# Decay products folded into q and k in place, in the scan of a three-branch decoder layer

## The chip, the cores and the metric

The kernel runs on one core of a Trainium2 chip, as one launch. The metric is the device time of that launch in microseconds (us). Three runs of the kernel before gave 2731.2, 2731.36 and 2727.7 us; the median is 2731.2 us. One more execution was recorded by the hardware profiler, and all rows of the trace come from it.

## The reference, cut to what matters

One layer over 2048 tokens (16 meta tokens stand ahead of them) with model width 1024. A normalised input goes through one wide projection, and three causal mixers run side by side on its parts: stick-breaking attention, a gated delta rule, and HGRN2, the third branch. Each has 4 heads of 128 dimensions; their outputs are gated, projected, mixed and added to the input. The change lies in the third branch, whose recurrence is, for one head and one chunk (`g_c` holds the running sum of the logarithms of the decays):

```python
o_inter = einsum('bhcd,bhde->bhce', q_c * exp(g_c), state)
dec = exp(where(causal, g_c[:, :, :, None, :] - g_c[:, :, None, :, :], -inf))
a = einsum('bhid,bhjd,bhijd->bhij', q_c, k_c, dec)
o = o_inter + einsum('bhij,bhje->bhie', a, v_c)
state = state * exp(g_end)[:, :, 0, :, None] + einsum('bhcd,bhce->bhde', k_c * exp(g_end - g_c), v_c)
```

The weight between token i and an earlier token j is thus a sum over 128 dimensions of q times k times the product of all decays between them, and each dimension has decays of its own.

## The kernel before, in words

The 2048 tokens are worked off in four stages of `TQ` = 512 (the loop over `j` at the end of the kernel). Dimensions lie on the 128 partitions and tokens along the free dimension, so a head's q is a tile of 128 x 528 (16 columns for the meta tokens of the first stage). The projections are made in three fp32r passes per product (`mm3`, lines 176 to 178): high part times high part and the two cross terms. They are by far the most of the work on TensorE.

Within a stage, two streams of work are traced one into the other by `weave`. One is the dense stream (`dense_work`): projections, gates and output products. The other is a scan: `sb_scan` (attention), `gdn_scan`, and `hg_scan` for the third branch, called twice per stage, for heads 0 and 1 and for heads 2 and 3. Here these are called the first and the second scan of a stage; there are eight in all. A scan yields an estimate of its own time (5.0 for each level of `hg_scan`), and `weave` traces dense work for a proportional time before it goes on with the scan. The program is traced under a context that orders the instructions of every engine along a simulated timeline; the order is fixed before the run, and each engine works through its own queue in that order. `issue_after` ties a block of instructions behind a given one on its engine.

`hg_scan` makes the 128 x 128 weight matrices by doubling. At level `s` = 1, 2, 4, ..., 64 the tokens are seen in pairs of neighbouring blocks of `s` tokens, a left one (k) and a right one (q). The weights between them need k times the decays from its token to the end of the left block, and q times the decays from the start of the right block to its token. For these:

- `pf` holds for every token the product of decays from the start of its block to itself, and `sf` the product from the token after it to the end of its block. Both are doubled in place after each level (line 1216 for `pf`, line 1215 for `sf`; at level 1 `sf` is made by GpSimd, lines 1212 and 1213).
- At each level a fresh tile `kql` from the pool "S" (21 buffers) takes right halves q times `pf` (line 1143) and left halves k times `sf` (line 1147; at level 1 a copy of k by GpSimd, line 1145).
- The level's products, 16 matmuls per head of 32 x 32 (levels 1 to 32) or 4 of 64 x 64, go into one bank `z` (line 1152), head 1 ahead of head 0. Level 1 has 16 more per head, k times q, for the diagonal.
- VectorE takes the wanted entries out of `z` by a mask (line 1200), and ScalarE copies them into `AT` (lines 1187, 1194 and 1207).

After the last level, q times `pf` (line 1223) and k times `sf` (line 1225) are made for whole chunks of 128, the latter is transposed on TensorE and copied by ScalarE (line 1227), and four steps per head run the recurrence between the chunks: lines 1236 to 1239 on TensorE, the update of the state on line 1241, the copy of the output on line 1242. The output goes on as `ob` to the product of the third branch.

Of the kernel before, what the change touches and what calls it, by code (L numbers as in the profile page):

```python
# [11 lines left out]
ALU = mybir.AluOpType  # L12
# [3 lines left out]
P = 128  # L16
# [3 lines left out]
META = 16  # L20
# [19 lines left out]
def kernel(  # L40
# [21 lines left out]
    nc = tc.nc  # L62
# [13 lines left out]
    def nm(s):  # L76
        uid[0] += 1
        return f"{s}_{uid[0]}"
# [5 lines left out]
    def slot(tag, shape=(P, WQ), dt=F32, bufs=None):  # L84
        return pool.tile(list(shape), dt, tag=tag, name=nm(tag), bufs=bufs or BUFS[tag])
# [18 lines left out]
    def p_z():  # L104
        return ps_z.tile([P, 512], F32, tag="z", name=nm("z"))

    def p_tr():
        return ps_z.tile([P, 512], F32, tag="z", name=nm("tr"))
# [20 lines left out]
    def rsqrt(v, rows, cols):  # L129

        y = slot("nr", (P, 24), F32, 4)
        u = slot("nu", (P, 24), F32, 4)
        nc.gpsimd.tensor_scalar(u[:rows, :cols], v, EPS, None, ALU.add)  # L133
        nc.gpsimd.tensor_tensor(y[:rows, :cols], u[:rows, :cols], mhalf[:rows, :cols], ALU.pow)
        return y
# [242 lines left out]
    def to_tokens(src, pt):  # L378

        for n in range(NT):  # L380
            nc.tensor.transpose(pt[:, n * P : (n + 1) * P], src[:, META + n * P : META + (n + 1) * P], ident)  # L381
        return pt
# [744 lines left out]
    def hg_scan(j, hs, st):  # L1127

        pf, kk, qq, vt, gate = zip(*(st.pop(h) for h in hs))
        two = range(2)  # L1130
        sf = [slot("S") for _ in two]
        s = 1
        lv = 0
        while s < P:
            def v4(t):
                r_ = t[:, META:].rearrange("p (b two s) -> p b two s", two=2, s=s)
                return r_[:, :, 0], r_[:, :, 1]

            nb = TQ // (2 * s)
            kql = [slot("S") for _ in two]  # L1140
            for i in two:
                kl_, kr_ = v4(kql[i])
                nc.vector.tensor_mul(kr_, v4(qq[i])[1], v4(pf[i])[1])
                if s == 1:
                    nc.gpsimd.tensor_copy(kl_, v4(kk[i])[0])
                else:
                    nc.vector.tensor_mul(kl_, v4(kk[i])[0], v4(sf[i])[0])
            z = p_z()
            last = None

            def mm(dst, lh, rh):
                return nc.tensor.matmul(dst, lh, rh, start=True, stop=True).ins  # L1152


            for i in (1, 0):
                with ExitStack() as es:
                    if last is not None:
                        es.enter_context(tc.issue_after(last))
                    if s == 64:

                        for n in range(NT):
                            c, o = META + n * P, 64 * (n % 2)
                            m = 2 * i + n // 2
                            last = mm(
                                z[o : o + 64, m * 64 : m * 64 + 64], kql[i][:, c : c + 64], kql[i][:, c + 64 : c + P]
                            )
                    elif s == 32:
                        for n in range(NT):
                            for b in (0, 64):
                                c, o = META + n * P + b, b + 32 * (n % 2)  # L1170
                                m = 2 * i + n // 2
                                last = mm(
                                    z[o : o + 32, m * 32 : m * 32 + 32], kql[i][:, c : c + 32],
                                    kql[i][:, c + 32 : c + 64],
                                )
                    else:

                        pairs = [(kql[i], kql[i])] + ([(kk[i], qq[i])] if s == 1 else [])
                        for q, (lh, rh) in enumerate(pairs):
                            for n in range(NT):  # L1180
                                for b in range(0, P, 32):
                                    c = META + n * P + b
                                    m = 2 * NT * q + NT * i + n
                                    last = mm(z[b : b + 32, m * 32 : m * 32 + 32], lh[:, c : c + 32], rh[:, c : c + 32])
            if s == 64:
                for g in two:
                    nc.scalar.copy(
                        AT[:64, :, g::2, 64:],
                        z[64 * g : 64 * g + 64, :256].rearrange("p (i n c) -> p i n c", i=2, n=2),
                    )  # L1190
            elif s == 32:
                for b in (0, 64):
                    for g in two:
                        nc.scalar.copy(
                            AT[b : b + 32, :, g::2, b + 32 : b + 64],
                            z[b + 32 * g : b + 32 * g + 32, :P].rearrange("p (i n c) -> p i n c", i=2, n=2),
                        )
            else:
                for q in range(2 if s == 1 else 1):
                    nc.vector.copy_predicated(  # L1200
                        AD, lvl[:, lv + 5 * q : lv + 5 * q + 1].broadcast_to([P, 2 * NT, 32]),
                        z[:, 256 * q : 256 * q + 256].rearrange("p (m c) -> p m c", c=32),
                    )
                if s == 16:
                    for b in range(4):
                        sl = slice(32 * b, 32 * b + 32)
                        nc.scalar.copy(AT[sl, :, :, sl], AD[sl].rearrange("p (i n) c -> p i n c", i=2))
            for i in two:
                pl_, pr_ = v4(pf[i])
                fl_, fr_ = v4(sf[i])  # L1210
                if s == 1:
                    nc.gpsimd.tensor_copy(fl_, pr_)
                    nc.gpsimd.memset(fr_, 1.0)
                else:
                    nc.vector.tensor_mul(fl_, fl_, pr_[:, :, s - 1 : s].broadcast_to([P, nb, s]))
                nc.vector.tensor_mul(pr_, pr_, pl_[:, :, s - 1 : s].broadcast_to([P, nb, s]))
            s *= 2
            lv += 1
            yield 5.0
        qe, ke, ket, os_ = [], [], [], []  # L1220
        for i in two:
            qe.append(slot("S"))
            nc.vector.tensor_mul(qe[i][:, META:], qq[i][:, META:], pf[i][:, META:])
            ke.append(slot("S"))
            nc.vector.tensor_mul(ke[i][:, META:], kk[i][:, META:], sf[i][:, META:])
            ket.append(slot("S", (P, NT, P)))
            nc.scalar.copy(ket[i].rearrange("p a b -> p (a b)"), to_tokens(ke[i], p_tr()))
            os_.append(slot("S"))
        ssq = slot("ssq", (P, 2 * NT), F32, 3)
        yield 4.0  # L1230
        for n in range(NT):
            cs = slice(META + n * P, META + (n + 1) * P)
            for i, h in enumerate(hs):
                p1 = p_tr()
                dst = p1[:, :P]
                nc.tensor.matmul(dst, qe[i][:, cs], Sh[h], start=True, stop=False)
                nc.tensor.matmul(dst, AT[:, i, n], vt[i][:, n], start=False, stop=True)  # L1237
                pS = p1[:, P : 2 * P]
                nc.tensor.matmul(pS, ket[i][:, n], vt[i][:, n], start=True, stop=True)
                e = META + (n + 1) * P - 1  # L1240
                nc.vector.scalar_tensor_tensor(Sh[h], Sh[h], pf[i][:, e : e + 1], pS, ALU.mult, ALU.add)
                nc.vector.tensor_copy(os_[i][:, cs], dst)
                junk = slot("junk", (P, P), F32, 2)
                m = NT * i + n
                nc.scalar.activation(
                    junk, os_[i][:, cs], AF.Square, scale=HD ** -0.5, accum_out=ssq[:, m : m + 1]
                )
                yield 1.5
        r = rsqrt(ssq, P, 2 * NT)
        yield 16.0  # L1250
        res = []
        for i in two:
            for n in range(NT):
                cs = slice(META + n * P, META + (n + 1) * P)
                m = NT * i + n
                nc.vector.tensor_scalar(os_[i][:, cs], os_[i][:, cs], r[:, m : m + 1], None, ALU.mult)
            res.append(put_ob(to_tokens(os_[i], p_tr()), gate[i]))
        return res
# [176 lines left out]
    with tc.issue_after(marks["act"]), tc.issue_after(marks["dve"]), tc.issue_after(marks["pool"]):  # L1435
# [47 lines left out]
        Sh = [const.tile([P, HD], F32, name=f"Sh{h}") for h in range(H)]  # L1483
# [123 lines left out]
```

## Time and profile before

| | |
|---|---|
| Profiled execution, device time | 2731.59 us |
| its span, first to last instruction | 2729.8 us |
| Median of three runs | 2731.2 us |
| TensorE matmul (PE) busy | 2693.7 us, 99% of the span |
| TensorE weight load (PEld) busy | 2245.8 us, 82% |
| VectorE (DVE) busy | 1433.1 us, 52% |
| ScalarE (ACT) busy | 960.2 us, 35% |
| GpSimd (POOL) busy | 718.8 us, 26% |
| Granted TensorE clock, mean | 0.998 |

Busy time is the time in which an engine has at least one instruction under way, so two that overlap count once; the mean of a group of instructions is that of their own durations. A row of a group ends with the idle time of its engine just ahead of it and with what ended that idle time. In rows that are ordered by time, the first number is the start and the second the length, both in us, and a number in square brackets is the idle time ahead.

### The profile page before, as it was taken

To read this page: it belongs to the slowest core of one execution; us is meant where nothing else is said; L and a number is where in the kernel's file an instruction comes from. 1 tells how busy PE (TensorE), PEld (TensorE's weight loads), DVE (VectorE), ACT (ScalarE), POOL (GpSimd) and SP (SyncE) were. 2 spreads that over 40 slices of the span, in tenths; PEclk is the share of its full clock that TensorE was granted. 3 is DMA by queue.
4 is the path that set the end of the run, shared out by engine and by line. 5 is a ranking of instruction groups with operands and counts; after the bars stand their busy time and mean duration, and the time that the engine had idled before them with its cause. 6 is when DMAs were issued, how large, how long until landed. Compare 5 with 4: busy or idle time off the path is not lost.

```text
span 2729.8 us, 46703 instructions
## 1 busy us (share of the span) xinstructions
PE 2693.7 (99%) x17984; PEld 2245.8 (82%) x17984; DVE 1433.1 (52%) x2878; ACT 960.2 (35%) x2207; POOL 718.8 (26%) x990
## 2 busy tenths in 40 slices
PE   7999999999999999999999999999999999999999
PEld 7998788888888888888888888888888887787887
DVE  5466647745357634443255765553325568556422
ACT  5564343343346212212144641321214456313120
POOL 4555213333133401112122332111212233302111
PEclk9999999999999999999999999999999999999999
DMA  7677756679654654557755456355764454554556
GB/s 261 221 235 251 250 184 221 231 268 319 197 180 146 206 176 130 157 160 242 230 188 171 156 171 203 107 156 155 253 217 142 163 169 142 161 161 121 162 162 212
DMA packets 201986, 521.08 MB, mean 191 GB/s; under 512 B 42976, under 2 KB 47008, under 8 KB 201764
## 3 DMA queue, kind: packets, MB, share of 16 engines
q1 hardware_dynamic: 201476, 518.03, 59.1%
q8 instruction: 142, 2.33, 0.3%
q14 instruction: 80, 0.66, 0.1%
q10 hardware_dynamic: 288, 0.07, 0.0%
HBM read 397.57 MB, written 120.44 MB: 190 GB/s over the span
## 4 chain that ended last, share of the span: by engine, by line
PE 93%; DVE 4%; DMA 1%; ACT 1%; issue 1%; POOL 0%; SPq 0%; DVEq 0%; POOLq 0%; ACTq 0%
PE acc L176 20%; PE acc L177 20%; PE acc L178 20%; PE av L176 5%; PE av L177 5%; PE av L178 5%; PE tr L559 2%; PE t L381 2%; PE z L1152 1%; PE z L176 1%; PE z L177 1%; PE z L178 1%; PE tr L381 1%; PE z L856 1%; PE tr L1237 1%
## 5 line engine op out<-in xcount | busy, mean ns | idle before, releaser
L176 PE MATMUL acc<-xh,w 128*128 128x512 f32 (+2 forms) x2096 | 796.8, 380 | 5.6 <-DVE y L1285 1.7
L177 PE MATMUL acc<-xl,w 128*128 128x512 f32 (+2 forms) x2096 | 790.7, 377 | 0.3 <-DVE xl L261 0.3
L178 PE MATMUL acc<-xh,w 128*128 128x512 f32 (+2 forms) x2096 | 787.1, 376 | 0.5 <-DVE w L127 0.5
L176 PEld LDWEIGHTS acc<-xh,w 128*128 128x128 f32 x2096 | 396.6, 189 | 75.2 <-DVE y L1285 2.1
L178 PEld LDWEIGHTS acc<-xh,w 128*128 128x128 f32 x2096 | 396.6, 189 | 66.8 <-DVE w L127 0.7
L177 PEld LDWEIGHTS acc<-xl,w 128*128 128x128 f32 x2096 | 396.4, 189 | 65.0 <-DVE xl L261 1.1
L531 DVE TENSOR_TENSOR_SCAN S<-S,zero 128x128 f32<-128x128 f32 (+4 forms) x216 | 199.1, 924 | 115.3 <-ACT S L525 105.1
L127 POOL TENSOR_TENSOR w<-wraw,w 128x512 fp32r<-128x512 f32 x106 | 147.0, 1390 | 236.2 <-ACT w L156 227.7
L537 POOL TENSOR_TENSOR S<-S,S 128x256 f32<-128x256 f32 (+2 forms) x108 | 96.5, 893 | 366.6 <-DVE S L531 196.6
L176 PE MATMUL av<-xh,w 128*128 128x512 f32 (+2 forms) x440 | 172.7, 392 | 0.0
L177 PE MATMUL av<-xl,w 128*128 128x512 f32 (+2 forms) x440 | 171.8, 390 | 0.0
L178 PE MATMUL av<-xh,w 128*128 128x512 f32 (+2 forms) x440 | 171.3, 389 | 0.0
L156 ACT CAST w<-wraw 128x512 fp32r<-128x512 f32 x182 | 112.5, 619 | 143.7 <-PE acc L178 69.9
L525 ACT ACTIVATE S<-z,rq 128x128 f32<-128x128 f32 (+4 forms) x216 | 117.1, 542 | 117.7 <-PE z L178 90.6
L737 DVE SCALAR_TENSOR_TENSOR D<-D,cw,D 128x512 f32<-128x512 f32 (+1 forms) x144 | 119.7, 838 | 21.3 <-ACT D L735 19.8
L127 DVE TENSOR_TENSOR S<-tr,S 128x512 fp32r<-128x512 f32 (+4 forms) x176 | 105.9, 606 | 42.5 <-ACT S L564 24.0
L1289 POOL TENSOR_TENSOR y<-y,g 128x512 f32<-128x512 f32 x32 | 48.2, 1506 | 288.8 <-DVE g L1287 288.8
L176 PE MATMUL acc<-ob,w 128*128 128x512 f32 x296 | 118.2, 400 | 1.4 <-ACT ob L402 1.4
L177 PE MATMUL acc<-ob,w 128*128 128x512 f32 x296 | 117.7, 398 | 0.0
L178 PE MATMUL acc<-ob,w 128*128 128x512 f32 x296 | 117.5, 397 | 0.0
L526 ACT ACTIVATE S<-z,rq 128x128 f32<-128x128 f32 (+4 forms) x216 | 116.8, 541 | 0.0
L133 POOL TENSOR_SCALAR nu<-nv 128x8 f32<-128x8 f32 (+3 forms) x39 | 14.8, 379 | 334.9 <-DVE nv L1057 194.4
(404 smaller groups left out, 4980.3 us busy)
## 6 DMA issues: line engine op xcount, KB each, us to landing
w<-wk SPq DMA_DIRECT2D x555, 512.0 KB, 3.6
wk<-w SPq DMA_DIRECT2D x184, 512.0 KB, 3.5
wraw<-in_w_in_dram SPq DMA_DIRECT2D x142, 256.0 KB, 4.0
D<-in_xq_dram SPq DMA_DIRECT2D x56, 256.0 KB, 4.4
S<-rows SPq DMA_DIRECT2D x48, 256.0 KB, 5.1
S<-dv SPq DMA_DIRECT2D x48, 256.0 KB, 4.7
out_dram<-D SPq DMA_DIRECT2D x32, 256.0 KB, 4.7
S<-dk SPq DMA_DIRECT2D x24, 264.0 KB, 3.9
```

The source lines that it names most:

```text
L127: (eng or nc.gpsimd).tensor_sub(out_, a, hi.bitcast(F32))
L156: nc.scalar.copy(hi, raw)
L176: nc.tensor.matmul(dst, lh, rh, start=first, stop=False)
L177: nc.tensor.matmul(dst, lh, rl, start=False, stop=False)
L178: nc.tensor.matmul(dst, ll, rh, start=False, stop=last)
L381: nc.tensor.transpose(pt[:, n * P : (n + 1) * P], src[:, META + n * P : META + (n + 1) * P], ident)
L525: nc.scalar.activation(pc[:, :n], z[:, :n], AF.Sigmoid, scale=rq[:, NT + i : NT + i + 1])
L526: nc.scalar.activation(at[:, :n], z[:, :n], AF.Sigmoid, scale=rq[:, i : i + 1])
L531: nc.vector.tensor_tensor_scan(pc[:, 0:n][:, ::-1], pc[:, 0:n][:, ::-1], zero1.broadcast_to([P, n]), 1.0 if carry[i] is None else pc[:, n ...
L537: eng.tensor_mul(at[:, :n], at[:, :n], pc[:, 1 : n + 1])
L559: nc.tensor.transpose(tr[:kw, i * P : (i + 1) * P], ats[i][:, a - lo : a - lo + kw], ident)
L737: nc.vector.scalar_tensor_tensor(dst[:, c0:], raw[:, c0 + i : c0 + i + n], cw[:, ci, i : i + 1], dst[:, c0:], ALU.mult, ALU.add)
```

## The change

The tiles `sf`, `kql`, `qe` and `ke` are gone. `qf` starts as q times its decay. From then on each level multiplies in place: the left halves of k by the product of all decays of the right block, the right halves of `qf` by that of the left block. These products of whole blocks stand in a short array `tt`: 256 entries per head after the first level, 128 after the second, down to 4. At level 1 they are made from the decays `pf` themselves, which are no longer changed. All of these multiplications are VectorE's; the three GpSimd instructions per head are gone. The matmuls read k and `qf` directly, and the next level's multiplications overwrite what the level's matmuls read. The recurrence takes the chunk's decay from the last part of `tt`.

```diff
-        sf = [slot("S") for _ in two]
+        qf = [slot("S") for _ in two]
+        tt = [slot("S") for _ in two]
+        off, prev = 0, None
...
-            kql = [slot("S") for _ in two]
-            for i in two:
-                kl_, kr_ = v4(kql[i])
-                nc.vector.tensor_mul(kr_, v4(qq[i])[1], v4(pf[i])[1])
-                if s == 1:
-                    nc.gpsimd.tensor_copy(kl_, v4(kk[i])[0])
-                else:
-                    nc.vector.tensor_mul(kl_, v4(kk[i])[0], v4(sf[i])[0])
+            if s == 1:
+                for i in two:
+                    nc.vector.tensor_mul(qf[i][:, META:], qq[i][:, META:], pf[i][:, META:])
...
-                        pairs = [(kql[i], kql[i])] + ([(kk[i], qq[i])] if s == 1 else [])
+                        pairs = [(kk[i], qf[i])] + ([(kk[i], qq[i])] if s == 1 else [])
...
             for i in two:
-                pl_, pr_ = v4(pf[i])
-                fl_, fr_ = v4(sf[i])
-                if s == 1:
-                    nc.gpsimd.tensor_copy(fl_, pr_)
-                    nc.gpsimd.memset(fr_, 1.0)
-                else:
-                    nc.vector.tensor_mul(fl_, fl_, pr_[:, :, s - 1 : s].broadcast_to([P, nb, s]))
-                nc.vector.tensor_mul(pr_, pr_, pl_[:, :, s - 1 : s].broadcast_to([P, nb, s]))
+                tl_, tr_ = v4(pf[i]) if s == 1 else (prev[i][:, 0::2, None], prev[i][:, 1::2, None])
+                kl_ = v4(kk[i])[0]
+                qr_ = v4(qf[i])[1]
+                nc.vector.tensor_mul(kl_, kl_, tr_.broadcast_to([P, nb, s]))
+                nc.vector.tensor_mul(qr_, qr_, tl_.broadcast_to([P, nb, s]))
+                nc.vector.tensor_mul(tt[i][:, off : off + nb, None], tl_, tr_)
+            prev = [t[:, off : off + nb] for t in tt]
+            off += nb
...
-            qe.append(slot("S"))
-            nc.vector.tensor_mul(qe[i][:, META:], qq[i][:, META:], pf[i][:, META:])
-            ke.append(slot("S"))
-            nc.vector.tensor_mul(ke[i][:, META:], kk[i][:, META:], sf[i][:, META:])
             ket.append(slot("S", (P, NT, P)))
-            nc.scalar.copy(ket[i].rearrange("p a b -> p (a b)"), to_tokens(ke[i], p_tr()))
+            nc.scalar.copy(ket[i].rearrange("p a b -> p (a b)"), to_tokens(kk[i], p_tr()))
...
-                nc.tensor.matmul(dst, qe[i][:, cs], Sh[h], start=True, stop=False)
+                nc.tensor.matmul(dst, qf[i][:, cs], Sh[h], start=True, stop=False)
...
-                e = META + (n + 1) * P - 1
-                nc.vector.scalar_tensor_tensor(Sh[h], Sh[h], pf[i][:, e : e + 1], pS, ALU.mult, ALU.add)
+                nc.vector.scalar_tensor_tensor(Sh[h], Sh[h], prev[i][:, n : n + 1], pS, ALU.mult, ALU.add)
```

The matmuls of levels 32 and 64 change their operands in the same way.

More of the change, by code (lines that the diff above doesn't have):

```diff
@@ L1164, in hg_scan @@
                             last = mm(
-                                z[o : o + 64, m * 64 : m * 64 + 64], kql[i][:, c : c + 64], kql[i][:, c + 64 : c + P]
+                                z[o : o + 64, m * 64 : m * 64 + 64], kk[i][:, c : c + 64], qf[i][:, c + 64 : c + P]
                             )
@@ L1172, in hg_scan @@
                                 last = mm(
-                                    z[o : o + 32, m * 32 : m * 32 + 32], kql[i][:, c : c + 32],
-                                    kql[i][:, c + 32 : c + 64],
+                                    z[o : o + 32, m * 32 : m * 32 + 32], kk[i][:, c : c + 32],
+                                    qf[i][:, c + 32 : c + 64],
                                 )
                     else:
-                        pairs = [(kql[i], kql[i])] + ([(kk[i], qq[i])] if s == 1 else [])
+                        pairs = [(kk[i], qf[i])] + ([(kk[i], qq[i])] if s == 1 else [])
                         for q, (lh, rh) in enumerate(pairs):
@@ L1219, in hg_scan @@
             yield 5.0
-        qe, ke, ket, os_ = [], [], [], []
+        ket, os_ = [], []
         for i in two:
-            qe.append(slot("S"))
-            nc.vector.tensor_mul(qe[i][:, META:], qq[i][:, META:], pf[i][:, META:])
-            ke.append(slot("S"))
-            nc.vector.tensor_mul(ke[i][:, META:], kk[i][:, META:], sf[i][:, META:])
             ket.append(slot("S", (P, NT, P)))
-            nc.scalar.copy(ket[i].rearrange("p a b -> p (a b)"), to_tokens(ke[i], p_tr()))
+            nc.scalar.copy(ket[i].rearrange("p a b -> p (a b)"), to_tokens(kk[i], p_tr()))
             os_.append(slot("S"))
```

## The prediction

> **What bounds the kernel now.** I read the page first: busy times, then the chain that ended last.
>
> ```profile
> span 2729.8 us, 46703 instructions
> PE 2693.7 (99%) x17984; PEld 2245.8 (82%) x17984; DVE 1433.1 (52%) x2878; ACT 960.2 (35%) x2207; POOL 718.8 (26%) x990
> PE 93%; DVE 4%; DMA 1%; ACT 1%; issue 1%; POOL 0%; SPq 0%; DVEq 0%; POOLq 0%; ACTq 0%
> ```
>
> TensorE is idle for 2729.8 - 2693.7 = 36.1 us in all, so no relief of another engine can be worth more unless TensorE gets less to do. Next I cut out the stretches of the eight scans that change. The columns are the stretch, its length, the busy time (and count) of PE, PEld, DVE, ACT and POOL, the granted clock, the DMA share and GB/s. The last three rows are from a finer cut, around the attention scan of the last stage.
>
> ```profile
> 420.00:460.00 40.00, 40.00 (x591) 32.01 (x590) 37.78 (x78) 12.01 (x27) 17.40 (x16) 1.00 0.57 194
> 510.00:560.00 50.00, 50.00 (x641) 40.05 (x640) 34.47 (x74) 17.90 (x39) 19.63 (x14) 1.00 0.72 252
> 1078.00:1108.00 30.00, 30.00 (x520) 22.93 (x519) 29.44 (x66) 4.29 (x8) 12.06 (x12) 1.00 0.50 148
> 1156.00:1206.00 50.00, 50.00 (x626) 39.56 (x625) 27.89 (x66) 8.19 (x19) 4.35 (x3) 1.00 0.56 164
> 1760.00:1800.00 40.00, 38.42 (x590) 30.70 (x589) 33.19 (x73) 10.00 (x23) 10.54 (x10) 1.00 0.46 135
> 1836.00:1886.00 50.00, 50.00 (x626) 39.56 (x625) 27.88 (x66) 8.77 (x20) 4.35 (x3) 1.00 0.56 161
> 2480.00:2515.00 35.00, 33.44 (x561) 26.34 (x560) 32.63 (x71) 8.43 (x19) 10.54 (x10) 1.00 0.46 136
> 2556.00:2606.00 50.00, 50.00 (x626) 39.54 (x625) 27.89 (x66) 8.60 (x20) 4.36 (x3) 1.00 0.54 162
> ...
> 2240.00:2260.00 20.00, 18.62 (x106) 15.37 (x105) 14.09 (x24) 11.86 (x29) 5.74 (x14) 1.00 0.35 117
> 2320.00:2340.00 20.00, 17.16 (x102) 13.87 (x101) 14.42 (x31) 13.02 (x31) 4.08 (x12) 0.98 0.34 102
> 2340.00:2360.00 20.00, 16.86 (x89) 13.65 (x88) 9.06 (x11) 3.50 (x10) 8.69 (x14) 0.93 0.47 141
> ```
>
> VectorE is nearly full in the first scans of the stages (29.44 of 30, 32.63 of 35), and yet TensorE is never idle in six of the eight stretches: dense matmuls fill it. In the other two it idles 40.00 - 38.42 = 1.58 and 35.00 - 33.44 = 1.56 us. The view of TensorE's waits puts this down to the scan itself:
>
> ```profile
> PE z L1152 <- DVE S L1143: 2.2, 2, 1.2
> ```
>
> Two waits, 2.2 us together: that is all of the 36.1 us that the scan's multiplications cause directly.
>
> **The change part by part.** First VectorE's own time. The groups of the scan, and two stretches of its timeline where nothing disturbs it:
>
> ```profile
> L1216 DVE TENSOR_TENSOR D<-D 128x256 f32<-128x256 f32 x112 | 54.5, 487 | 0.6 <-POOL S L1212 0.6
> L1143 DVE TENSOR_TENSOR S<-D,D 128x256 f32<-128x256 f32 x112 | 52.5, 471 | 0.1
> L1215 DVE TENSOR_TENSOR S<-S,D 128x256 f32<-128x256 f32 x96 | 47.7, 497 | 0.0
> L1147 DVE TENSOR_TENSOR S<-D,S 128x256 f32<-128x256 f32 x96 | 44.9, 468 | 0.0
> L1225 DVE TENSOR_TENSOR S<-D,S 128x512 f32<-128x512 f32 x16 | 14.2, 887 | 0.0
> L1223 DVE TENSOR_TENSOR S<-D,D 128x512 f32<-128x512 f32 x16 | 14.2, 886 | 0.0
> ```
> ```profile
> 1770.25 0.41 DVE L1143 TENSOR_TENSOR S<-D,D 128x256 f32<-128x256 f32 x1
> 1770.59 0.41 DVE L1147 TENSOR_TENSOR S<-D,S 128x256 f32<-128x256 f32 x1
> ...
> 1788.72 0.68 DVE L1223 TENSOR_TENSOR S<-D,D 128x512 f32<-128x512 f32 x1
> 1789.32 0.68 DVE L1225 TENSOR_TENSOR S<-D,S 128x512 f32<-128x512 f32 x1
> ```
>
> From start to start a 256-column product takes 0.34 us (1770.25 to 1770.59; 0.335 over longer runs) and a 512-column one 0.60. Removed, per head: 112/16 + 96/16 + 96/16 + 112/16 = 26 products of 256 columns and 2 of 512, which is 26 x 0.335 + 2 x 0.60 = 9.9 us. Added, per head: one of 512 (the start of `qf`), two of 256 at each of 7 levels, and the seven of `tt` with 256, 128, ..., 4 columns. The short ones are in no row. They lie between nothing and 0.335 us each; the line through 0.335 at 256 and 0.60 at 512 columns gives 0.07 + 0.00104 per column, an estimate of 1.0 us for the seven, and I take it. Together 0.60 + 14 x 0.335 + 1.0 = 6.3 us. Saved: 3.6 us per head, x16 = 58 us of VectorE. Strides and factors read again and again cost no more than before: line 1216 already multiplies in place with a broadcast factor at all seven levels.
>
> What is that worth on TensorE? Its matmuls are the same in number and shape, so its 2693.7 us stay, and the 58 us lie beside them, as in the six stretches without idle time. The gain that follows from the rows is the 2.2 us of waits.
>
> GpSimd loses its three instructions per head:
>
> ```profile
> L1212 POOL COPY S<-D 128x256 f32<-128x256 f32 x16 | 8.5, 530 | 0.0
> L1145 POOL COPY S<-D 128x256 f32<-128x256 f32 x16 | 7.2, 469 | 19.8 <-DVE D L1084 15.7 <-PE tr L381 4.1
> L1213 POOL MEMSET S<- 128x256 f32 x16 | 5.3, 331 | 0.0
> ```
>
> That is 21.0 us of an engine that is busy 26% of the time: nothing on the path. The scan also takes 8 buffers of "S" in place of 24 out of 21. In the groups above VectorE was held up 0.1 us ahead of line 1143, the writer of `kql`; so I count nothing for that.
>
> The **added wait** matters most. Before, lines 1143 to 1216 never waited for matmuls; in 1770.25 to 1789.32 they run on while TensorE is still levels behind. After, the products of a level overwrite what its matmuls read, so VectorE waits for TensorE at each level and TensorE for VectorE at the next. The rows that size it, from a second scan, are the starts of level 2 to 64 on TensorE and one mask copy behind its matmuls:
>
> ```profile
> 1860.64 0.76 PE L1152 MATMUL z<-S 128*32 128x32 f32 x64
> 1865.02 0.76 PE L1152 MATMUL z<-S 128*32 128x32 f32 x64
> 1868.68 0.76 PE L1152 MATMUL z<-S 128*32 128x32 f32 x64
> 1873.05 0.76 PE L1152 MATMUL z<-S 128*32 128x32 f32 x64
> 1877.41 0.46 PE L1152 MATMUL z<-S 128*32 128x32 f32 x32
> 1880.77 0.69 PE L1152 MATMUL z<-S 128*64 128x64 f32 x16
> ```
> ```profile
> 1181.34 0.76 PE L1152 MATMUL z<-S 128*32 128x32 f32 x64
> 1182.14 0.45 DVE L1200 COPY_PREDICATED AD<-lvl,z 128x256 f32<-128x256 uint8 x1 [1.03 <-PE z L1152]
> ```
>
> Between the end of one level and the start of the next TensorE has 2.9 (1877.87 to 1880.77) to 3.6 us (1861.40 to 1865.02) of dense matmuls. The new turn-round: 0.04 us until the mask copy starts (1181.34 + 0.76 to 1182.14), 0.34 for it, 4 x 0.335 for the products, two of `tt` at 0.1 to 0.2, and about 0.1 for the last one's end and the signal: 2.0 to 2.2 us, and 1.8 at the last levels, where ScalarE copies. So it fits with 0.7 us or more to spare. The work queued behind a waiting product is VectorE's evacuation of dense results; waits of this kind were there before, at the mask copy, and TensorE did not idle for them. Bounds: 0 where the order leaves 3 us, and where it puts a level straight behind the one before, 2.2 us at 6 transitions of 8 scans, 106 us. The order is made with these waits known, and dense work is at hand, so I take the value near 0.
>
> At the start, `qf` takes 1.20 us for two heads where two of line 1143 took 0.67. At the end, the transposes wait for the last matmuls and three products more, some 1 us. Both lie beside dense matmuls, since the steps between chunks wait for TensorE's order anyway:
>
> ```profile
> 1799.02 0.35 DVE L1241 SCALAR_TENSOR_TENSOR Sh<-Sh,D,tr 128x128 f32<-128x128 f32 x1 [4.99 <-PE tr L1239]
> ```
>
> What the turn-round can lose its 0.7 us to is GpSimd:
>
> ```profile
> 1764.97 4.41 POOL L127 TENSOR_TENSOR ob<-S,ob 128x512 fp32r<-128x512 f32 x3
> 1768.16 1.50 DVE L1147 TENSOR_TENSOR S<-D,S 128x256 f32<-128x256 f32 x1
> ```
>
> While GpSimd subtracts, a product takes 1.50 in place of 0.41 us, 1.1 us late. Over all scans the groups' means above 0.41 (0.68 for 512 columns) add up to 8.6 + 6.8 + 8.4 + 5.6 + 3.3 + 3.3 = 36 us of such lateness, of which TensorE saw at most 2.2. [...]
>
> **The sum.** The profiled execution took 2731.59 us, 0.4 above the median of the runs. 2731.6 - 2.2 for the two waits + 2.2, between 0 and 36, for late turn-rounds (they reach TensorE in about the measure in which lateness did so far) = 2731.6. I forecast **2731 us, no change**. About 0.2%, 5.5 us, is what a measurement of this kernel can tell from no change.
>
> **The rivals.** *Slower: the lead is lost.* Each time GpSimd's subtractions catch a product in a turn-round, the lateness goes to TensorE as soon as it is over the 0.7 us to spare. The place is the first scans, where GpSimd is busy 10.5 to 17.4 us of a stretch. If half of the 36 us get through, and the 2.2 are gone: 2731.6 - 2.2 + 18 = 2747; if a third, 2741. It is decided by whether a turn-round with one catch, 2.2 + 1.1 = 3.3 us, finds less dense work than that. For it: two of the five gaps shown are 2.9 us. Against it: the other three are 3.6, and catches are fewer with 14 products per head than with 26.
>
> *Faster: a new order also frees other waits.* The order of every engine is made anew, and the three rows of the last attention scan show 1.38 + 2.84 + 3.14 = 7.4 us of idle time, and a clock of 0.98 and 0.93, worth 20 x (0.02 + 0.07) = 1.8 us. Without these and the 2.2: 2731.6 - 11.4 = 2720. For it: an attention scan with the same code in other stages has none. Against it: none of that work is touched.
>
> *It doesn't do what it says:* products with the factor read from every second entry of a short array run slower, at 0.68 us say, as for 512 columns. The turn-round is then 2.2 + 4 x 0.34 = 3.6 us, 0.7 over two of the five gaps, so 0.28 on average at 48 transitions: 2731.6 - 2.2 + 13 = 2743. Line 1216 speaks against it.
>
> **How the numbers follow.** No change 0.58, lost lead 0.19, faster 0.20, slow products 0.03. The likeliest gives 2731, with 2726 to 2737 as its own range. To leave out no more than 2 in 10 the range goes down to the whole of the faster case, 2720, and up to the milder half of the lost lead, 2742. Faster by over 0.2% has 0.20, within 0.2% 0.58, slower 0.22.
>
> **What would show it.** In the profile after: PE busy within a few us of 2693.7; VectorE's busy time in each of the eight stretches down by about 7 us (58/8) and its new products 0.41 us long; no GpSimd copies in the scan; the matmuls of a level 2 us or more behind those of the one before, with no idle time ahead. Idle time of TensorE ahead of line 1152's matmuls, released by VectorE and over 8 us in sum, would make the forecast wrong on the slow side; idle time gone around 2250 to 2350 us, on the fast side.

## The result and the profile after

The changed kernel takes 2740.85 us (median of 6 runs) where the kernel before takes 2729.01 on the same chip (6 runs): a ratio of 1.0046, with a 95% interval of 1.0036 to 1.0056. It is slower by 12 us, twice what this measurement can tell from no change. The profiled execution took 2744.88 us; its page says:

```profile
span 2742.9 us, 46622 instructions
PE 2700.3 (98%) x17984; PEld 2250.5 (82%) x17984; DVE 1382.4 (50%) x2782; ACT 960.7 (35%) x2207; POOL 690.4 (25%) x942
```

VectorE does 1433.1 - 1382.4 = 50.7 us less, GpSimd 28.4 us less, TensorE runs the same 17984 matmuls, and yet the span is 13.1 us longer. Of these, 6.5 us are idle time of TensorE (2742.9 - 2700.3 = 42.6 in place of 36.1), and 6.6 us are a longer busy time of the same matmuls.

Five of the eight scans' stretches after the change, in the columns of the prediction; where the scan has moved, the stretch is moved with it:

```profile
420.00:460.00 40.00, 40.00 (x615) 33.27 (x614) 29.35 (x65) 14.06 (x32) 15.04 (x11) 1.00 0.65 224
...
1078.00:1108.00 30.00, 29.48 (x465) 22.52 (x465) 20.39 (x44) 4.72 (x8) 8.79 (x6) 1.00 0.48 143
1156.00:1206.00 50.00, 49.99 (x611) 39.67 (x610) 18.87 (x50) 5.67 (x11) 3.97 (x3) 1.00 0.55 168
1760.00:1800.00 40.00, 37.79 (x498) 30.07 (x497) 24.30 (x65) 5.30 (x9) 10.34 (x7) 0.96 0.47 141
...
2485.00:2520.00 35.00, 32.77 (x478) 26.07 (x476) 22.16 (x60) 4.71 (x8) 9.66 (x7) 0.95 0.45 136
```

VectorE has more room in every one of them (22.16 of 35 us where it had 32.63). But TensorE now idles in three first scans: 0.52, 2.21 and 2.23 us. And its clock falls to 0.96 and 0.95 in two of these stretches, where it was 1.00. The second scan shown, and those left out, look untouched. TensorE's waits tell the rest; each row gives the sum, how many, and the longest:

```profile
PE z L1151 <- DVE D L1211: 5.0, 3, 2.2
PE acc L176 <- ACT D L1265: 3.5, 2, 2.5
PE acc L176 <- DVE D L1281: 2.1, 1, 2.1
```

The two waits of 2.2 us in sum ahead of line 1152 are gone, as forecast. In their place stand 5.0 us ahead of the same matmuls (now line 1151), and 3.5 + 2.1 us that no row of before had, at a place outside the scan. That is 10.6 - 2.2 = 8.4 us more. So there are two places to look at.

**First place: the start of a first scan.** The trace from 1768 us on (stage 2), GpSimd, VectorE, then TensorE:

```profile
1768.71 6.12 POOL L127 TENSOR_TENSOR ob<-S,ob 128x512 fp32r<-128x512 f32 x4 [7.08 <-ACT ob L402]
...
1769.69 2.58 DVE L1146 TENSOR_TENSOR S<-D,D 128x512 f32<-128x512 f32 x2
1772.19 2.93 DVE L1213 TENSOR_TENSOR S<-D 128x256 f32<-128x256 f32 x2
1775.04 1.58 DVE L1213 TENSOR_TENSOR S<-S 128x128 f32<-128x128 f32 x12
...
1776.88 0.42 DVE L1211 TENSOR_TENSOR D<-D,D 128x256 f32<-128x256 f32 x1
...
1777.35 0.46 PE L1151 MATMUL z<-S,D 128*32 128x32 f32 x32 [2.21 <-DVE D L1211]
```

Level 2 on TensorE waits for a product of k (line 1211) that starts at 1776.88. Ahead of it on VectorE stand the two starts of `qf`, the two first `tt` products, and all twelve shorter `tt` products (128 columns down to 4), which are needed only at later levels. At prices without disturbance that is 1.20 + 0.67 + 1.58 us, and 0.76 for two products of q and k: 4.2 us. It took 7.6 (1769.69 to 1777.30), because GpSimd makes four subtractions of the delta rule's output from 1768.71 to 1774.83, and `qf` and the first `tt` took 2.58 and 2.93 us meanwhile.

**Second place: the third branch's output product**, some 40 us behind the second scan. In the next rows `av` and `acc` are accumulators of dense products, line 402 makes the high part of the third branch's output, and lines 344 and 348 are the squares and sums of the next stage's input. Stage 1 after, ScalarE, VectorE, then TensorE:

```profile
1249.70 0.63 ACT L344 ACTIVATE D<-D 128x512 f32<-128x512 f32 x1 [5.08 <-DMA D<-in_xq_dram]
1250.24 0.60 ACT L402 CAST ob<-S 128x512 fp32r<-128x512 f32 x1
...
1257.85 0.60 ACT L1265 ACTIVATE D<-acc 128x512 f32<-128x512 f32 x1 [0.23 <-DVE D L348]
...
1251.47 7.08 DVE L348 TENSOR_TENSOR D<-D,D 128x512 f32<-128x512 f32 x7 [1.99 <-ACT D L344]
...
1258.50 0.50 PE L176 MATMUL acc<-xh,w 128*128 128x512 f32 x1 [2.49 <-ACT D L1265]
```

And the same of before, ScalarE:

```profile
1242.73 0.62 ACT L402 CAST ob<-S 128x512 fp32r<-128x512 f32 x1 [5.66 <-DVE S L399]
...
1243.74 0.61 ACT L402 CAST ob<-S 128x512 fp32r<-128x512 f32 x1
1247.24 0.63 ACT L344 ACTIVATE D<-D 128x512 f32<-128x512 f32 x1 [2.89 <-DMA D<-in_xq_dram]
```

Before, both casts were done (1244.35) when the first square began (1247.24). After, the first cast comes 7.5 us later, at 1250.24, and the squares are in their place by then. They hold up the gate's activation (line 1265) on ScalarE, and seven sums in one row hold up the product with the accumulator (line 1281) on VectorE. No accumulator comes free, and TensorE stands 2.49 us. Waits of this kind end at 605.77 (2.13 us) and 1943.91 (1.05 us) too. GpSimd has a part in it that no run separates: it subtracts for the same late outputs at 1250.92 and 1252.72 (1.29 and 1.30 us), and the two sums of line 348 that it meets take 1.30 and 1.70 us where the other five take 0.69, some 1.6 us more.

**Why the output is late.** The starts of level 1 and level 64 on TensorE, in the second scan of stage 1, before:

```profile
1176.44 0.46 PE L1152 MATMUL z<-S 128*32 128x32 f32 x32
...
1201.45 0.69 PE L1152 MATMUL z<-S 128*64 128x64 f32 x16
```

After, with level 2 and level 4 between them, and VectorE's first product behind level 4:

```profile
1178.34 0.46 PE L1151 MATMUL z<-S,D 128*32 128x32 f32 x32
...
1183.36 0.76 PE L1151 MATMUL z<-S,D 128*32 128x32 f32 x64
...
1188.89 0.76 PE L1151 MATMUL z<-S,D 128*32 128x32 f32 x64
...
1210.90 0.69 PE L1151 MATMUL z<-S,D 128*64 128x64 f32 x16
...
1189.43 0.42 DVE L1211 TENSOR_TENSOR D<-D,S 128x256 f32<-128x256 f32 x1 [3.77 <-PE z L1151]
```

Seven levels took 25.0 us from first to last start and now take 32.6; they also start 1.9 us later. The levels are 5.5 us apart (1183.36 to 1188.89) where they were 3.4 to 4.9. The turn-round itself is no longer than forecast: VectorE stands idle for 3.77 us up to 1189.43, so its last product for level 4 ended at 1185.66, 1.5 us behind the matmuls of level 2 (1184.12), and 3.2 us before level 4 starts. The spacing is that of the planned order, not a delay on the chip.

**The slower clock.** Stretches of 10 us after:

```profile
1250.00:1260.00 10.00, 7.51 (x30) 5.74 (x29) 7.91 (x10) 6.33 (x11) 2.59 (x2) 0.95 0.97 341
1260.00:1270.00 10.00, 10.00 (x42) 8.08 (x41) 2.46 (x5) 1.82 (x3) 3.80 (x4) 0.88 0.36 109
1770.00:1780.00 10.00, 7.79 (x181) 5.96 (x180) 9.30 (x24) 1.03 (x2) 4.83 (x4) 0.89 0.18 54
1780.00:1790.00 10.00, 10.00 (x163) 7.79 (x162) 4.19 (x8) 0.00 (x0) 2.58 (x2) 0.94 0.52 159
600.00:610.00 10.00, 7.87 (x28) 6.02 (x27) 9.42 (x12) 5.48 (x10) 2.41 (x3) 0.85 0.58 217
...
2500.00:2510.00 10.00, 8.36 (x121) 6.69 (x122) 7.18 (x24) 0.00 (x0) 2.57 (x2) 0.83 0.32 96
```

Each of the four waits of 2.1 to 2.5 us is followed by a granted clock that costs 10 x (0.05 + 0.12), 10 x (0.11 + 0.06), 10 x (0.15 + 0.02, the 0.02 in the next stretch) and 10 x 0.17 us, which is 1.7 us each. Added up over the 10-us stretches up to the last instruction, 1 minus the granted clock is worth 5.9 us before and 11.9 after. These 6.0 us are most of the 6.6 us by which the matmuls became longer. With the 8.4 us of waits that makes 14.4. Waits elsewhere are 1.9 us shorter (8.4 - 6.5), and 0.6 us of the longer matmuls stay without a cause: 13.1.

### The profile page after: what moved, and what is told of

The parts are those of the page before. It is cut to its first block, busy times and chain, and to the rows that moved or that the text cites. A ratio compares the mean times of both kernels' runs of the same rounds, so it can differ in the third digit from the quotient of the medians.

```text
span 2742.9 us, 46622 instructions
## 1 busy us (share of the span) xinstructions
PE 2700.3 (98%) x17984; PEld 2250.5 (82%) x17984; DVE 1382.4 (50%) x2782; ACT 960.7 (35%) x2207; POOL 690.4 (25%) x942
## 4 chain that ended last, share of the span: by engine, by line
PE 92%; DVE 4%; DMA 1%; ACT 1%; issue 1%; POOL 0%; SPq 0%; DVEq 0%; ACTq 0%; POOLq 0%
PE acc L176 20%; PE acc L177 20%; PE acc L178 20%; PE av L177 5%; PE av L176 5%; PE av L178 5%; PE tr L559 2%; PE t L381 2%; PE z L1151 1%; PE z L176 1%; PE z L177 1%; PE z L178 1%; PE z L856 1%; PE tr L381 1%; DVE D L348 1%
## 5 line engine op out<-in xcount | busy, mean ns | idle before, releaser
L127 POOL TENSOR_TENSOR w<-wraw,w 128x512 fp32r<-128x512 f32 x106 | 140.6, 1329 | 250.7 <-ACT w L156 219.0
L127 DVE TENSOR_TENSOR S<-tr,S 128x512 fp32r<-128x512 f32 (+4 forms) x176 | 106.0, 607 | 42.6 <-ACT S L564 24.0
L559 PE MATMUL tr<-ident,S 128*128 128x128 f32 (+1 forms) x608 | 100.7, 272 | 0.8 <-DVE S L537 0.8
```

Source lines behind the costliest of these rows:

```text
L127: (eng or nc.gpsimd).tensor_sub(out_, a, hi.bitcast(F32))
L559: nc.tensor.transpose(tr[:kw, i * P : (i + 1) * P], ats[i][:, a - lo : a - lo + kw], ident)
```

## The experiments

Two theories stood against each other for the loss. **The lost lead:** GpSimd's subtractions catch VectorE's products at the start of a first scan, and the `tt` products make it worse (this is the prediction's slow rival). **The spacing:** the new wait makes the planned levels lie further apart, and the late output meets the next stage's squares. The expectations call these theories A and B; theory C is a loss spread over all levels. The first four kernels tell them apart.

**e1_sub_on_vector**: the low part of the delta rule's output is subtracted by VectorE, so GpSimd no longer makes it at the start of a first scan.

```diff
-    def put_ob(src_ps, gate):
+    def put_ob(src_ps, gate, eng=None):
...
-        sub_lo(ol, t[:, META:], oh)
+        sub_lo(ol, t[:, META:], oh, eng)
...
-            res.append(put_ob(to_tokens(os_[h], p_tr()), st[h]["gate"]))
+            res.append(put_ob(to_tokens(os_[h], p_tr()), st[h]["gate"], nc.vector))
```

> The changed kernel, with the low parts of the second branch's four outputs subtracted by VectorE instead of GpSimd, so that GpSimd is still at the start of a stage's first scan. Theory A (at the start of the first scans GpSimd catches the start of qf and the first products of block decays, so level 2 comes too late for TensorE): the three waits of TensorE ahead of level 2 (0.5, 2.2 and 2.2 us) go, and with the last two the slow clock after them, about 1.4 us each: 5 to 8 us less than the changed kernel, about 2733 to 2736. Theory B (only the waits at the third branch's product matter): no gain, or 1 to 2 us of loss from 4 x 0.6 us more on VectorE. Theory C (the loss is spread over all levels, by matmuls of a level that are cut into halves): no gain.

Measured: 2733.77 us, ratio 1.0018 [1.0008, 1.0027]. From the view of TensorE's waits:

```profile
PE acc L176 <- ACT D L1265: 2.9, 2, 1.8
...
PE z L1151 <- DVE D L1211: 0.8, 2, 0.5
```

The waits at the first place fall from 5.0 to 0.8 us, those at the second stay (2.9 us for line 1265, and 2.1 for line 1281 as before this edit). 1.0046 - 1.0018 = 0.0028, or 7.6 us, came with this edit. The order on VectorE changed with it, though: in stage 2, two of the twelve short `tt` products are left ahead of the first product of k for level 2 (line 1211, at 1772.92), so e1 does not tell the catch by GpSimd from the queue of `tt` products. And the kernel is still slower than before, so the lost lead is not the whole.

**e2_squares_later**: the squares and their sums are traced one projection later; nothing in the scan is touched.

```diff
-        tot = None
-        for k in range(KC):
...
+        tot = []
...
+        def squares():
+            for k in range(KC):
...
+            later(sums)
...
-        later2(sums)
-        return xt, rb
...
+        later(squares)
+        return xt, tot
```

> The changed kernel, with the squares and sums of the next stage's input traced one projection later, so behind that projection's gate on ScalarE. Theory B (the second scan ends later than before, and its outputs then meet the squares and sums of the next stage on ScalarE and VectorE, so the gate and the product that free TensorE's accumulators come late): the three waits at the third branch's product in stages 0, 1 and 2 (2.1, 2.5 and 1.0 us) go, and the slow clock after the first two: 5 to 9 us less than the changed kernel, about 2732 to 2736. Theory A alone: no gain. Theory C: no gain.

Measured: 2733.63 us, ratio 1.0022 [1.0012, 1.0031]. TensorE's waits, and ScalarE at the output of stage 1 (line 405 is line 402 of the changed kernel):

```profile
PE z L1154 <- DVE D L1214: 5.0, 3, 2.2
```
```profile
1241.77 1.22 ACT L405 CAST ob<-S 128x512 fp32r<-128x512 f32 x2 [4.28 <-DVE S L402]
```

The mirror image of e1: the first place keeps its 5.0 us, and both rows of the second place are gone. The second scan itself is as long as in the changed kernel (32.5 us from level 1 at 1171.25 to level 64 at 1203.72), so the longer scan costs little once its output meets no squares. 0.0024, or 6.5 us, hang on the squares lying where the late output comes.

**e3_one_kql**: the kernel before, with one pair of `kql` for all levels. A level's products now overwrite what the level's matmuls read: the change's new wait alone, with all products and GpSimd's copies of before.

```diff
         sf = [slot("S") for _ in two]
+        kql = [slot("S") for _ in two]
...
             nb = TQ // (2 * s)
-            kql = [slot("S") for _ in two]
```

> The kernel before, with kql as one pair of tiles written again at each level in place of a fresh pair. Nothing else changes: the same products, the same GpSimd copies. Only the new wait is there, VectorE for TensorE at each level. If that wait is what makes the scan longer (levels 5.5 us apart in place of 3.6 to 4.4) and so makes the second scan's outputs late: levels about 5 to 6 us apart, the last output of the second scan some 5 us later, and 4 to 12 us more than before, 2733 to 2741. If instead the buffers of q and of the decays, which come free early in the changed kernel, move the next stage's loads and squares: no more than 2 us from before.

Measured: 2740.38 us, ratio 1.0039 [1.0027, 1.0052]. TensorE's waits, and levels 2 and 4 in the second scan of stage 1:

```profile
PE acc L176 <- DVE D L1287: 4.8, 3, 1.6
PE tr L381 <- DVE S L1225: 2.2, 1, 2.2
```
```profile
1184.01 0.76 PE L1152 MATMUL z<-S 128*32 128x32 f32 x64
...
1189.54 0.76 PE L1152 MATMUL z<-S 128*32 128x32 f32 x64
```

The wait alone is enough for a loss about as large as the whole change's (the intervals overlap), and for the 5.5 us between levels. It isn't the same sum, though: no wait ahead of the scan's own matmuls is left here, and in place of the first place's 5.0 us there are more waits at the output product and one at the transposes of k.

**e4_levels_earlier**: the changed kernel, whose scan says 3.5 us per level to the tracer in place of 5.0, so less dense work is traced between two levels.

```diff
-            yield 5.0
+            yield 3.5
```

> The changed kernel, with 3.5 in place of 5.0 as the estimate that the scan gives for a level, so that a third less dense work is traced between two levels. If the distance of 5.5 us between levels is set by when the planner holds the products for ready, it stays above 5 us, and the time is that of the changed kernel within 3 us. If it is set by the dense work traced between, it falls to about 4 us, the second scan ends 8 us or more earlier, and the waits at the third branch's product go: 5 to 9 us less.

Measured: 2743.75 us, ratio 1.0052 [1.0039, 1.0065]. Level 2 and level 4 start at 1182.49 and 1188.04 us, again 5.5 us apart, and the waits at both places stay (5.2 us at the first, 3.5 and 1.7 at the second). The spacing does not come from how much dense work is traced between levels.

**e5_both**: the edits of e1 and e2 together, on the changed kernel.

> The changed kernel with both edits: the second branch's subtractions on VectorE and the squares one projection later. If the two groups of waits are the whole loss and don't depend on each other, the gains add up: 1.0018 + 1.0022 - 1.0046 = 0.9994 of the kernel before, within 0.9985 to 1.0005. If a third part of the loss stays (the halves of a level's matmuls, the evacuations queued behind a waiting product), it stays above 1.0010. If the 58 us less on VectorE were worth something of their own, it is below 0.9985.

Measured: 2723.75 us, ratio 0.9984 [0.9976, 0.9993] against 2728.38 of the kernel before: faster than both kernels, by 4.6 and about 17 us. That is a little more than the two gains added up to, and just past the 0.9985 below which VectorE's relief was to be worth something of its own; the interval leaves both open. TensorE's waits:

```profile
PE z L1154 <- DVE D L1214: 0.8, 2, 0.5
...
PE acc L176 <- DVE y L1282: 0.3, 1, 0.3
```

Of the changed kernel's loss and of the waits it was put down to, nothing is left, so the two places together are the cause. In the profiled executions, the gain on the kernel before is in waits too. Beside the 2.2 us ahead of line 1152, that kernel had these:

```profile
PE z L944 <- DVE S L928: 2.0, 1, 2.0
PE acc L176 <- DVE y L1285: 1.7, 1, 1.7
...
PE acc L176 <- DMA w<-wk: 1.0, 2, 0.5
```

In e5 the first and the last are below 0.2 us, the second is 0.3, and the scan's are 0.8: 2.0 + 1.0 + 1.4 + 1.4 = 5.8 us less. TensorE's idle time is 30.6 us (2721.7 - 2691.1) where it was 36.1. Three of the four lie outside the scan, and that they fell by these edits is not shown: in the changed kernel the second is 0.3 us and the third below 0.2 already, and the first differs between two executions of that kernel, 1.7 us here and 0.5 in e10.

**e6_both_on_before**: the same two edits on the kernel before, to see whether they gain by themselves.

> The kernel before with the same two edits, to see what they are worth without the change. If they only mend what the change brought, it is within 0.1% of the kernel before (0.999 to 1.001); the 2.2 us of waits ahead of level 32 may go, which is the lower end. If they are worth as much here as in the changed kernel, it is 0.995 to 0.996.

Measured: 2727.84 us, ratio 0.9999 [0.9990, 1.0007]. They don't. The waits ahead of level matmuls rise from 2.2 to 3.4 us, with the added subtractions on a VectorE that is full in the first scans. So the gain of e5, 2723.75 us on the same chip, needs the change.

**e7_decays_last**: the changed kernel, with every `tt` product issued behind the level's products of k and q.

```diff
-                nc.vector.tensor_mul(qr_, qr_, tl_.broadcast_to([P, nb, s]))
-                nc.vector.tensor_mul(tt[i][:, off : off + nb, None], tl_, tr_)
+                qm = nc.vector.tensor_mul(qr_, qr_, tl_.broadcast_to([P, nb, s])).ins
+                with tc.issue_after(qm):
+                    nc.vector.tensor_mul(tt[i][:, off : off + nb, None], tl_, tr_)
```

> The changed kernel, with the products of a level's block decays issued behind the products of k and q of that level on VectorE (in the profile, the twelve small ones stand 1.6 us long ahead of the first products of k and q that TensorE waits for). If they are a part of the late level 2, the three waits of TensorE ahead of level 2 fall from 5.0 us to 2 or less, and with the slow clock gone after two of them the time falls by 3 to 7 us. If GpSimd's hold on VectorE makes it late alone, nothing changes, within 2 us.

Measured: 2734.55 us, ratio 1.0029 [1.0019, 1.0039]. The waits ahead of the scan's matmuls fall to 0.9 us, with GpSimd's subtractions still made there; those at the second place stay (3.4 and 2.1 us). In stage 2 the two starts of `qf` are still caught (2.58 us from 1764.64), so the catch alone does not make level 2 late enough: the `tt` products, which stand in the queue without need, are a part of it. That these alone would not do it either, no run shows. By the prices above their 4.2 us from 1769.69 would have ended at 1773.9, before TensorE fell idle at 1775.14.

**e8_one_kql_squares_later**: e3 with the squares of e2.

> The kernel before with kql as one pair of tiles (ratio 1.0039 alone) and the squares one projection later. If the loss that the wait alone brings is the meeting of the late second scan with the next stage's squares, most of it goes: 1.0000 to 1.0015, and TensorE no longer waits ahead of the matmuls that follow the third branch's first products. If it is spread over the levels, it stays at 1.003 or more.

Measured: 2732.0 us, ratio 1.0015 [1.0006, 1.0024]. The waits on line 1287 that e3 had (line 1290 here) fall from 4.8 to 0.8 us, and 0.0024 of the ratio with them, the same as from the changed kernel to e2. The one wait of 2.2 us at the transposes remains. The second place is thus made by the new wait alone.

**e9_all_three**: the edits of e1, e2 and e7 together.

> The changed kernel with all three edits: subtractions on VectorE, squares one projection later, block decays behind the products of k and q. With GpSimd already out of the way at the start of a first scan, only 0.5 us of waits ahead of level 2 is left there, so the third edit can give at most that: 0.9975 to 0.9990 of the kernel before, not to be told from the two edits (0.9984).

Measured: 2726.26 us, ratio 0.9994 [0.9985, 1.0003], short of what was expected and not better than e5. The first place had no more to give; in its trace a wait of 1.4 us has come inside the delta rule's scan, where e5 has 0.3. That row differs between executions of one kernel as well: 0.2 us in the changed kernel's first profile and 1.4 in that of e10.

**e10_changed_again**: the changed kernel, beside e9.

> The changed kernel itself, beside the one with three edits on the same chip: 1.0036 to 1.0056 of the kernel before, as it was measured first.

Measured: 2743.23 us, ratio 1.0049 [1.0037, 1.0062], in line with the first result.

## Why the prediction was wrong

It said "no change", 2731 us with 2726 to 2737 as its own range. The time is 2740.85, within the wide range of 2720 to 2742, but the interval of the ratio excludes its forecast. By its own steps:

- **What the engines do** held. The products take 0.42 us, so the factors from the short array cost nothing extra and that rival is out. The twelve short `tt` products of two heads take 1.58 us, 0.79 per head, in place of 0.68 by the prediction's line. PE has the same matmuls, and the copies on GpSimd are gone. VectorE saved 50.7 in place of 58 us.
- **The lateness through GpSimd** hardly fell, and here "catches are fewer with 14 products per head than with 26" was wrong. The groups after:

```profile
L1211 DVE TENSOR_TENSOR D<-D,S 128x256 f32<-128x256 f32 x96 | 50.0, 521 | 72.7 <-PE z L1151 72.7
L1212 DVE TENSOR_TENSOR S<-S,S 128x256 f32<-128x256 f32 x96 | 44.5, 463 | 0.0
...
L1146 DVE TENSOR_TENSOR S<-D,D 128x512 f32<-128x512 f32 x16 | 19.4, 1245 | 0.1
L1213 DVE TENSOR_TENSOR S<-D 128x256 f32<-128x256 f32 x16 | 13.7, 896 | 0.0
...
L1211 DVE TENSOR_TENSOR D<-D,D 128x256 f32<-128x256 f32 x16 | 11.0, 690 | 0.0
```

  Above 0.42 (0.68 for 512 columns) these are 9.7 + 4.1 + 9.0 + 7.6 + 4.3 = 35 us of lateness, where it was 36 before. And 21 of them lie on the first instructions of a scan, the last three groups: a start of `qf` takes 1.245 us on average, and 0.805 in e1, where VectorE makes the subtractions.
- **The added wait** is the step that failed: "The order is made with these waits known, and dense work is at hand, so I take the value near 0." The turn-round was shorter still than forecast (1.5 us measured between levels 2 and 4, against 2.0 to 2.2), and it fits. But the order, made with the wait known, put the levels 5.5 us apart, and a scan that takes 7.6 us longer is not free just because TensorE stays full during it. What is late next wasn't asked: the output at lines 399 and 402, which runs into the next stage's squares on two other engines. No rival had this place. The runs give it 0.0024 of the ratio, 6.5 us (e2, and e8 against e3).
- **"2.2, between 0 and 36, for late turn-rounds"** was mis-sized: 5.0 us measured. The rival "the lead is lost" named the mechanism and the place, the first scans, and its milder price of 2741 is the measured time, but by luck. No third of 36 us came through at many turn-rounds; level 2 alone was hit, at the start of the scan. The place is worth 7.6 us by e1, 4.6 by e7. The other half of the loss came from the second place. The step "`qf` takes 1.20 us for two heads ... lie beside dense matmuls" left out the catch (2.58 us) and the `tt` products, which were counted as work but not as a queue ahead of level 2.
- **The clock** was no term of the sum. After the four waits at the two places it costs 1.7 us each; over the whole span it costs 6.0 us more than before.
- **The faster rival**, "a new order also frees other waits", came true in part in the changed kernel, beside the larger losses: the wait on line 1285, which lay in the rival's stretch from 2340 to 2360 us, falls from 1.7 to 0.3 us, and the 1.0 us on `w` is gone. The rest of its 7.4 us of idle time stays.
- **The sign it gave for itself** was too narrow. Idle time ahead of the scan's matmuls stayed at 5.0 us, below the 8 named; more than half of the new idle time was elsewhere.

**What stays open:** why the planned order puts levels with the new wait 5.5 us apart although VectorE is done 3 us earlier (e4 only excludes the traced share of dense work); what the 0.0015 that e8 keeps consists of, beside its wait of 2.2 us; how much of the second place's hold-up is GpSimd's; and whether another order of the same kernel would have gained as e5 did.

## What to carry to other kernels

A buffer rewritten in place ties producer and consumer together at each step. Even when the turn-round is hidden, ask when the last step ends now, and what its output meets on the engines that take it on. And when two small edits cure one place each, measure them together: here the change became a gain of 0.16% (0.9984, with an interval up to 0.9993) only after both meetings were gone, and e9, with one edit more, can't be told from the kernel before.

## What the runs showed of the hardware

The granted clock fell after waits shorter than I had thought worth pricing, 1.33 to 2.49 us long. TensorE after the wait of 2.21 us:

```profile
1778.76 0.63 PE L178 MATMUL av<-ob,w 128*128 128x512 f32 x1
1779.18 0.63 PE L176 MATMUL av<-ob,w 128*128 128x512 f32 x1
...
1781.48 0.39 PE L177 MATMUL acc<-ob,w 128*128 128x512 f32 x1
1781.70 0.39 PE L178 MATMUL acc<-ob,w 128*128 128x512 f32 x1
```

Dense matmuls of 512 columns start 0.42 to 0.43 us apart in place of 0.22 to 0.23, and the slow stretch lasts 3.5 us (from 1777.74 to 1781.25); the 2.13, 2.23 and 2.49 us waits are followed by lower clocks as well (0.85, 0.83 and 0.88 in the stretches above). The wait of 1.05 us at 1943.91 is not (1.00 from 1940 to 1950), and neither is one of 1.15 us in the kernel before, which ends at 1785.59 (1.00 from 1780 to 1790). But the length of a wait does not decide it. In the other profile of the changed kernel (e10), the wait that was 2.13 us long comes again with 2.12 us, ends at 606.69, and the clock stays full:

```profile
600.00:610.00 10.00, 7.88 (x34) 6.12 (x33) 9.58 (x13) 5.40 (x10) 2.93 (x3) 1.00 0.61 227
```

And in the first profile a wait of only 1.33 us, which ends at 240.30, is followed by a clock of 0.83 from 240 to 250 us. So 1.7 us is what a fall of the clock costs here, and a wait of this length does not always bring one. What decides which waits are followed by it, no run here shows.
